# Opening of a two-layer hybrid decoder trunk: the first half's first projections on h times the norm weight, the norm factor multiplied into the products, and 44 matmuls on a constant ahead

## The chip, the cores and the metric

The kernel runs on one core of a Trainium2 chip. TensorE (PE in the profile; PEld is its weight load) multiplies matrices into PSUM, eight banks of 512 float32 numbers per partition. VectorE (DVE), ScalarE (ACT) and GpSimd (POOL) work on tiles of 128 partitions; SyncE (SP) issues transfers. The engines run beside each other and wait for each other by semaphores; each takes its own instructions in order. The metric is the device time of one execution in microseconds, lower is better.

## The reference

Two layers, each a mixer and a feed-forward sub-layer with RMS norms around both. 16 learned tokens are put ahead of 512, so L = 528 and D = 1024. The part that the change touches is the head of the first mixer:

```python
def rms_norm(x, g):
    y = xf * lax.rsqrt(jnp.mean(xf * xf, axis=-1, keepdims=True) + RMS_EPS)
    return y * g
...
u = rms_norm(h, pre_g)
z = jnp.einsum("bld,de->ble", u, w_in)
q, k, v, f_logit, a_val, a_gate, sc_b, sc_c, sc_x = jnp.split(z, idx, axis=-1)
...
a = a_val * jax.nn.sigmoid(a_gate)
a = causal_depthwise_conv(a, a_dw_w) + a_dw_b
...
y_sc = sc_b * causal_depthwise_conv(sc_c * sc_x, sc_conv_w)
```

The rest of a layer is an attention with forget gates (8 heads), a head norm, an output projection, a post norm, and a gated feed-forward part with a short convolution; everything is computed in float32.

## The kernel before

All activations lie transposed: a tile `[128, 8, 528]` holds feature 128 k + p in partition p and block k. `h` is such a tile. The 528 tokens are worked in two halves of H = 264; `hf` is the half. To get float32 accuracy, both operands of a product are split into a high part (rounded by a cast) and a low part (the rest), and each product is three matmuls, high x high, low x high, high x low (`mm3`). `uhi` and `ulo` are the two parts of the normed input u, `whi` and `wlo` those of a weight block of 128 output columns (8 x 128 x 128 numbers, 512 KB; `raw` is the loaded block, in a ring of three buffers). A weight block costs a transfer on SP's queue, a cast on ACT (L617) and a subtraction on DVE (L621); its raw buffer is free when the subtraction is done.

The order of all instructions is set while the program is built, by a planner (`Flow`): work is handed to it with a duration, a priority and what it waits for, and it lets each engine take what can start first, by priority among what is ready. PE is fed by generators ("threads") that yield what they wait for. The resulting order on each engine is fixed in the program.

The opening, under the pool `pre`, does this in the kernel before:

- `load_h` asks for h in four transfers for each half (pairs of blocks k), weight blocks 0, 1 and 2 come between the halves, the next ones as raw buffers come free. The parameters of both layers (`pv`) are two transfers on POOL's queue; DVE makes `pg` from each (L407).
- ACT squares pairs of blocks of h (`Norms.square`, L723), DVE adds them up, and PE multiplies the sum with a matrix of 1/D (`om_d`, L772), which gives the mean square in all partitions. ACT and DVE make the factor of it (L782 to L793).
- ACT multiplies h with the norm weight into `hg` (`gained`, L802), DVE multiplies by the factor (L814), ACT casts to `uhi` (L816) and DVE subtracts to `ulo` (L817), pair by pair.
- `first_half` then runs the first six weight blocks on the first half: blocks 0 and 1 together, k by k, then 2, 3, 4 and 5 together. Blocks 0 and 1, and 2 and 3, are gate and value of the two tiles of the convolution module, 4 and 5 are `sc_c` and `sc_x` of the short convolution.

The mixer starts with `gated` for the first half (the sigmoid by exp, ln and exp on ACT, then a product with the value on DVE into `apad`), runs the same six blocks on the second half (`firsts`: 0 and 1, then 2 and 3, then 4 and 5), and starts the 31 taps of the convolution on DVE (`tap`, L932). Behind these 288 first products comes the value projection (L1183), and from there projections, attention and convolution are interleaved.

Of the kernel before, what the change touches and what calls it, by code (L numbers as in the profile page):

```python
# [13 lines left out]
ALU = mybir.AluOpType  # L14
# [35 lines left out]
NP = 6  # L50

# [304 lines left out]
def tile_hybrid_trunk(ctx: ExitStack, tc: tile.TileContext, xT, wflat, pv_d, out):  # L356
# [46 lines left out]
    for l in range(DEPTH):  # L403
        pv = T(const, [P, NPV], F32, f"pv{l}")
        nc.gpsimd.dma_start(pv, pv_d[l])
# [254 lines left out]
    class First:  # L660
# [8 lines left out]

        def steps(self, hf, *group):  # L670
# [218 lines left out]
    def mixer(l, ypool, first, close_first, spans):  # L889
# [7 lines left out]

        mp = ms.enter_context(tc.tile_pool(name=f"mp{l}", bufs=1, reuse_waits="tile"))
# [6 lines left out]
        conv, apads, sigs = [], [], []  # L905
        for j in range(2):
            sigs.append(T(mp, [P, L], F32, ("sccx", "cxp")[j]))
            apad = T(mp, [P, L + CK - 1], F32, "apad", 2)
            nc.gpsimd.memset(apad[:, :CK - 1], 0.0)
            apads.append(apad)  # L910
            conv.append(T(mp, [P, L], F32, "cacc", 2))
        gated_at = {}

        def gated(hf, j, tok):
            c = half_sl(hf)
            sig = sigs[j][:, c]
            us = act_us(H)
            a = a0 = act(us, lambda: nc.scalar.activation(sig, first.ps[hf, 2 * j], AF.Exp, scale=-1.0), tok)
            b = act(us, lambda: nc.scalar.activation(sig, sig, AF.Ln, bias=c_one), a)
            b = act(us, lambda: nc.scalar.activation(sig, sig, AF.Exp, scale=-1.0), b)  # L920
            gated_at[hf, j] = got = dve(dve_us(H), lambda: nc.vector.tensor_mul(
                apads[j][:, CK - 1 + H * hf:CK - 1 + H * (hf + 1)], first.ps[hf, 2 * j + 1], sig), b, prio=0)
            for i in range(2):
                first.slot[hf, 2 * j + i].close(a0, got)
# [31 lines left out]
        for j in range(2):  # L956
            gated(0, j, first.tok[0, 2 * j + 1])
# [6 lines left out]
        def sc_c(j):  # L964
            t = sc[j] = T(mp, [P, L], F32, "sccx")

            def use(hf, ps, tok):
                c = half_sl(hf)
                sc_at[j, "c", hf] = act(act_us(H), lambda: nc.scalar.copy(t[:, c], ps), tok)
                return [sc_at[j, "c", hf]]  # L970

            return use

        def sc_x(j):
            t = sc[j]
            cx = T(mp, [P, L + 2], F32, "cxp")
# [37 lines left out]
        for i, make in ((4, sc_c), (5, sc_x)):  # L1014
            use = make(0)
            for hf in range(2):
                evacs += use(hf, first.ps[hf, i], first.tok[hf, 5])
# [935 lines left out]
```

## Time and profile before

| what | value |
|---|---|
| median of 3 runs | 1320.25 us (1317.92 to 1321.16) |
| the profiled execution | 1320.06 us |
| its span, first to last instruction | 1318.4 us |
| mean granted clock of TensorE | 0.997 |
| PE busy | 1278.1 us, 97% of the span |
| DVE, ACT, POOL busy | 859.1, 626.3, 98.9 us |
| bytes moved by the transfers | 118.26 MB, mean 90 GB/s |

A row of the timeline has the start and the duration in microseconds, the engine, the line of the kernel, the instruction, its output and inputs with their shapes, and how often it stands there in a row (then the duration is that of all); behind it, in brackets, the idle time of the engine and what ended it. A matmul's duration covers its way through the array, and matmuls overlap, so the distance between starts says how fast they go. A row on a line or tile has the shortest, the median and the longest duration in ns.

### The profile page before, as it was taken

Reading aid. Unit: us, or ns where it says so; the run is one execution under the profiler, and the core shown is the slowest. Engines: PE = TensorE matmul, PEld = TensorE weight load, DVE = VectorE, ACT = ScalarE, POOL = GpSimd, SP = SyncE. Lnnn points to the kernel's source line nnn. Section 1 sums busy time; section 2 is a strip of 40 time slices with the busy share of each in tenths; the row PEclk is TensorE's granted clock in tenths of the full one; section 3 lists DMA queues with packets and bytes.
Section 4 is the critical chain, followed back from the end, with each engine's and each line's share of the span. In section 5 each row is a group of like instructions: output and inputs, shape, how many; then the busy total and the mean of one; then the engine's idle time right before and its main releaser. Section 6 shows DMA issues by size and latency. Waiting matters only on the chain. (4 is left out here: it accounts for less than half of the span.)

```text
span 1318.4 us, 23824 instructions
## 1 busy us (share of the span) xinstructions
PE 1278.1 (97%) x9758; PEld 1223.3 (93%) x9758; DVE 859.1 (65%) x1450; ACT 626.3 (48%) x1176; POOL 98.9 (8%) x255
## 2 busy tenths in 40 slices
PE   5999999999999999999989999999999999999997
PEld 4989898999999999999989898979999799989997
DVE  6588856488633674576575888666877247646764
ACT  7345568555423432234662555685644233323353
POOL 1313321000000000000003223110000000000000
PEclk9999999999999999999989999999999999999999
DMA  7032120602222222223240322116032222232221
GB/s 247 21 98 75 56 75 33 213 30 85 92 97 81 97 86 91 96 86 106 82 163 17 99 82 65 57 54 214 24 97 85 92 97 95 71 108 97 90 71 65
DMA packets 42700, 118.26 MB, mean 90 GB/s; under 512 B 4848, under 2 KB 15088, under 8 KB 42592
## 3 DMA queue, kind: packets, MB, share of 16 engines
q1 hardware_dynamic: 42496, 116.48, 26.6%
q8 instruction: 77, 1.26, 0.4%
q0 software_dynamic: 96, 0.26, 0.1%
q14 instruction: 31, 0.25, 0.1%
HBM read 108.04 MB, written 4.33 MB: 85 GB/s over the span
## 5 line engine op out<-in xcount | busy, mean ns | idle before, releaser
L648 PE MATMUL psum<-uhi,whi 128*128 128x264 f32 (+1 forms) x1984 | 466.9, 288 | 7.4 <-ACT uhi L816 7.4
L648 PE MATMUL psum<-ulo,whi 128*128 128x264 f32 (+1 forms) x1984 | 461.7, 285 | 0.9 <-DVE ulo L817 0.9
L648 PE MATMUL psum<-uhi,wlo 128*128 128x264 f32 (+1 forms) x1984 | 459.7, 284 | 0.0
L648 PEld LDWEIGHTS psum<-uhi,whi 128*128 128x128 f32 x1984 | 333.4, 189 | 11.6 <-ACT uhi L816 8.6
L648 PEld LDWEIGHTS psum<-ulo,whi 128*128 128x128 f32 x1984 | 334.2, 190 | 1.9 <-DVE ulo L817 1.5
L648 PEld LDWEIGHTS psum<-uhi,wlo 128*128 128x128 f32 x1984 | 334.0, 190 | 0.0
L648 PE MATMUL psum<-yhi,whi 128*128 128x264 f32 (+3 forms) x840 | 235.2, 304 | 1.4 <-ACT yp L1885 1.0
L648 PE MATMUL psum<-ylo,whi 128*128 128x264 f32 (+3 forms) x840 | 232.6, 300 | 1.0 <-DVE ylo L1085 0.8
L648 PE MATMUL psum<-yhi,wlo 128*128 128x264 f32 (+3 forms) x840 | 231.7, 299 | 0.5 <-DVE wlo L621 0.5
L503 ACT CAST whi<-raw 128x1024 fp32r<-128x1024 f32 (+1 forms) x110 | 113.5, 1033 | 212.5 <-PE psum L648 198.9
L504 DVE TENSOR_TENSOR wlo<-raw,whi 128x1024 fp32r<-128x1024 f32 (+1 forms) x110 | 132.0, 1201 | 81.5 <-ACT whi L503 79.5
L648 PEld LDWEIGHTS psum<-yhi,whi 128*128 128x128 f32 x840 | 150.0, 188 | 10.2 <-ACT yp L1885 1.4
L648 PEld LDWEIGHTS psum<-ylo,whi 128*128 128x128 f32 x840 | 150.0, 188 | 7.5 <-DVE ylo L1085 2.0
L648 PEld LDWEIGHTS psum<-yhi,wlo 128*128 128x128 f32 x840 | 150.2, 188 | 6.1 <-DVE wlo L621 0.9
L1834 DVE SCALAR_TENSOR_TENSOR c<-z,pv,c 128x528 f32<-128x528 f32 (+1 forms) x176 | 132.2, 757 | 2.7
L621 DVE TENSOR_TENSOR wlo<-raw,whi 128x1024 fp32r<-128x1024 f32 (+2 forms) x86 | 102.5, 1207 | 43.0 <-ACT whi L617 42.5
L617 ACT CAST whi<-raw 128x1024 fp32r<-128x1024 f32 (+2 forms) x86 | 87.9, 1035 | 35.8 <-DMA raw<-in_w_dram 17.4
L932 DVE SCALAR_TENSOR_TENSOR cacc<-apad,pv,cacc 128x528 f32<-128x528 f32 x120 | 87.6, 773 | 0.5
L1852 ACT CAST yhi<-c 128x528 fp32r<-128x528 f32 (+1 forms) x44 | 27.6, 628 | 111.3 <-DVE c L1848 111.3
L1844 ACT ACTIVATE c<-c 128x528 f32<-128x528 f32 (+1 forms) x44 | 28.2, 640 | 81.7 <-DVE c L1834 81.7
L1832 ACT ACTIVATE c<-z,pv 128x528 f32<-128x528 f32 (+1 forms) x88 | 63.5, 728 | 0.0
L1797 DVE TENSOR_TENSOR z<-psum,rz 128x528 f32<-128x528 f32 x40 | 28.3, 709 | 53.7 <-PE psum L648 52.1
(199 smaller groups left out, 1422.1 us busy)
## 6 DMA issues: line engine op xcount, KB each, us to landing
raw<-in_w_dram SPq DMA_DIRECT2D x160, 512.0 KB
raw<-in_w_dram SPq DMA_DIRECT2D x32, 448.0 KB
h<-in_x_dram SPq DMA_DIRECT2D x16, 264.0 KB
raw<-in_w_dram SPq DMA_DIRECT2D x4, 528.0 KB
q<-q SPq DMA_DIRECT2D x16, 132.0 KB
k<-k SPq DMA_DIRECT2D x16, 132.0 KB
h_dram<-h SPq DMA_DIRECT2D x4, 528.0 KB
h<-h_dram SPq DMA_DIRECT2D x8, 264.0 KB
```

Of the source, the lines that this page charges most:

```text
L503: nc.scalar.copy(hi[:, :sz], raw[:, :sz])
L504: nc.vector.tensor_sub(lo[:, :sz], raw[:, :sz], hi[:, :sz].bitcast(F32))
L617: nc.scalar.copy(box["hi"][:, :sz], box["raw"][:, :sz])
L621: nc.vector.tensor_sub(lo[:, :sz], box["raw"][:, :sz], box["hi"][:, :sz].bitcast(F32))
L648: nc.tensor.matmul(d, lhsT=w[a][:, k, cols], rhs=rhs(b, k, hf), start=start and i == 0 and p == 0, stop=stop and i == n - 1 and p == 2)
L932: nc.vector.scalar_tensor_tensor(conv[j], in0=src, in1=conv[j], scalar=col("a_dw_w", CK * j + i), op0=ALU.mult, op1=ALU.add)
L1797: nc.vector.tensor_mul(two(t[:, off:]), srcs[0], two(rz))
L1832: nc.scalar.activation(dst, src[:, 2:2 + 2 * fw], AF.Copy, scale=wtap(2, t))
L1834: nc.vector.scalar_tensor_tensor(dst, in0=src[:, i:i + 2 * fw], scalar=wtap(i, t), in1=dst, op0=ALU.mult, op1=ALU.add)
L1844: silu = nc.scalar.activation(cs[0], cs[0], AF.Silu)
L1852: nc.scalar.copy(ghi, cs[0])
```

## The change

The first half's projections no longer wait for the norm factor. u = h x gain x factor, and the factor is one number for each token, thus for each column of the product; so the first half's six blocks are multiplied with the two parts of h x gain, and the factor `rz0` is multiplied into the products afterwards.

- High and low parts of h x gain for the first half are made straight from h, block by block: ACT scales into the high part, DVE takes the low part in one operation (`yhi`, `ylo`; they lie in tiles of the later `y`). The pool of these tiles and a new pool `mq0` are opened ahead.
- The six blocks run one after the other over all k (`First.alone`) instead of two or four together.
- `gated` and the use of `sc_c` multiply with `rz0` on DVE (lines 925, 932 and 1005 and 1006 of the changed kernel). `gated` for the first half is planned in the opening.
- u itself is still needed in both halves for later projections: DVE multiplies h by gain and factor in one operation per block (L1821), ACT casts (L1825) and DVE subtracts (L1827). The buffer `hg` is gone.
- 44 matmuls on a tile of ones stand at the head of PE's queue; the planner is told 8.0 us for them. Nothing reads their result.
- Layer 0's `pv` goes on SP's queue ahead of all, and weight block 0 ahead of h.

```diff
-        nc.gpsimd.dma_start(pv, pv_d[l])
+        (nc.gpsimd if l else nc.sync).dma_start(pv, pv_d[l])
...
+        def alone(self, hf, both, *ids):
+            slots = [(yield from flow.grab(pring[0]["mm" if both else "s"], self.slot[hf, ids[0]]))]
...
+            for j, i in enumerate(ids):
...
+                yield [self.ws[i].tok]
+                for k in range(KD):
+                    yield [When(lambda: self.at.get((hf, k)))]
+                    mm3({hf: self.ps[hf, i]}, self.ws[i].w, [k], self.rhs, start=k == 0, stop=k == KD - 1)
...
+        def gated(self, hf, j, tok, rz=None, rz_at=None):
...
+            if rz is not None:
+                a = b = dve(dve_us(H), lambda: nc.vector.tensor_mul(sig, gate, rz), tok, rz_at, prio=0)
...
+            if rz is not None:
+                b = dve(dve_us(H), lambda: nc.vector.tensor_mul(sig, sig, rz), b, prio=0)
...
+        warm = T(sp, [P, H], F32R, "warm", 1)
+        nc.vector.memset(warm.bitcast(F32), 1.0)
+        for i in range(WARM):
+            nc.tensor.matmul(psum[:, 7, :H], lhsT=warm[:, :P], rhs=warm, start=True, stop=True)
+        flow.pe += WARM_US
+        plan_w(1, -1)
         h, h_at = load_h(sp, xT)
...
-        hg, hg_at = T(sp, [P, KD, L], F32, "hg", 1), {}
+        for k in range(KD):
+            hk, hi, lo, gc = h[:, k, :H], u_raw[0][k], u_raw[1][k], g0[:, k:k + 1]
+            c = act(act_us(H) + 0.06, lambda hk=hk, hi=hi, gc=gc: nc.scalar.activation(hi, hk, AF.Copy, scale=gc),
+                    h_at[0, k - k % 2], prio=0)
+            d = dve(stt_us(H), lambda hk=hk, hi=hi, lo=lo, gc=gc: nc.vector.scalar_tensor_tensor(
+                lo, in0=hk, scalar=gc, in1=hi.bitcast(F32), op0=ALU.mult, op1=ALU.subtract), c, prio=0)
+            first.at[0, k] = [c, d]
...
+        def normed(hf, prio):
+            c = half_sl(hf)
+            key = ("h", hf)
+            yield from norms.factor(key, H, out=None if hf else rz0)
...
+        def opening():
+            for j in range(2):
+                yield from first.alone(0, True, 2 * j, 2 * j + 1)
+                front.gated(0, j, first.tok[0, 2 * j + 1], rz0, rz_at)
+            for i in (4, 5):
+                yield from first.alone(0, False, i)
...
-        flow.thread(first_half(first, False))
+        flow.thread(normed(0, 1.2))
+        flow.thread(normed(1, 0.7))
+        flow.thread(opening())
```

Where instructions stand now. On PE, the head of the queue before (`om_d` is the matrix of the mean, 161 and 168 are weight blocks 0 and 1):

```order
L772 MATMUL psum_67<-acc_137,om_d_88 128x264 x2
L648 MATMUL psum_67<-uhi_113,whi_161 128x264
L648 MATMUL psum_67<-ulo_114,whi_161 128x264
L648 MATMUL psum_67<-uhi_113,wlo_166 128x264
L648 MATMUL psum_67<-uhi_113,whi_168 128x264
```

and in the changed kernel (`whi_218` is weight block 0, `yhi_22` and `yhi_23` the high parts for k = 0 and 1):

```order
L1790 MATMUL psum_67<-warm_159 128x264 x44
L650 MATMUL psum_67<-yhi_22_126,whi_218 128x264
L650 MATMUL psum_67<-ylo_30_134,whi_218 128x264
L650 MATMUL psum_67<-yhi_22_126,wlo_224 128x264
L650 MATMUL psum_67<-yhi_23_127,whi_218 128x264
L650 MATMUL psum_67<-ylo_31_135,whi_218 128x264
```

The sum for the norm factor stood ahead of all products; now it stands in the middle of block 2, and that of the second half behind the first three products of block 4.

On DVE, between the second half's sum of squares and the second half's low parts, before:

```order
L732 TENSOR_TENSOR acc_189<-acc_189,c_261 128x528
L621 TENSOR_TENSOR wlo_314<-raw_243,whi_310 128x1056
L621 TENSOR_TENSOR wlo_331<-raw_272,whi_316 128x1056
L787 SCALAR_TENSOR_TENSOR rs_23_129<-psum_67,rs_23_129 128x264
L793 SCALAR_TENSOR_TENSOR rs_23_129<-rs_23_129 128x264
L814 TENSOR_TENSOR hg_130<-hg_130,rs_23_129 128x2x264 x3
L817 TENSOR_TENSOR ulo_114<-hg_130,uhi_113 128x2x264 x3
```

and in the changed kernel (`rz_44` is the first half's factor, `rs_47` the second half's; `sccx` and `cxp` hold the sigmoids of the two tiles):

```order
L623 TENSOR_TENSOR wlo_405<-raw_331,whi_393 128x1056
L925 TENSOR_TENSOR sccx_145<-psum_67,rz_44_153 128x264
L925 TENSOR_TENSOR cxp_149<-psum_67,rz_44_153 128x264
L802 SCALAR_TENSOR_TENSOR rs_47_206<-psum_67,rs_47_206 128x264
L1821 SCALAR_TENSOR_TENSOR h_205<-h_205,pg_3_70,rz_44_153 128x264
L808 SCALAR_TENSOR_TENSOR rs_47_206<-rs_47_206 128x264
L1821 SCALAR_TENSOR_TENSOR h_205<-h_205,pg_3_70,rz_44_153 128x264
L932 TENSOR_TENSOR sccx_145<-sccx_145,rz_44_153 128x264
L932 TENSOR_TENSOR cxp_149<-cxp_149,rz_44_153 128x264
L933 TENSOR_TENSOR apad_146<-psum_67,sccx_145 128x264
L933 TENSOR_TENSOR apad_150<-psum_67,cxp_149 128x264
L1821 SCALAR_TENSOR_TENSOR h_205<-h_205,pg_3_70,rs_47_206 128x264 x4
```

The first half's gating and its first two scalings of u moved in ahead of the second half's u, which begins with the last row. The remaining scalings and low parts of the first half's u stand behind those of the second half.

On SP's queue, the head before:

```order
L460 DMA h_128<-in_x_dram 128x2x264 x4
L613 DMA raw_135<-in_w_dram 128x1024
L613 DMA raw_140<-in_w_dram 128x1024
L613 DMA raw_147<-in_w_dram 128x1024
L460 DMA h_128<-in_x_dram 128x2x264 x4
```

and in the changed kernel:

```order
L407 DMA pv_2_68<-in_pv_dram 128x254
L615 DMA raw_207<-in_w_dram 128x1024
L462 DMA h_205<-in_x_dram 128x2x264 x4
L615 DMA raw_213<-in_w_dram 128x1024
L615 DMA raw_221<-in_w_dram 128x1024
L462 DMA h_205<-in_x_dram 128x2x264 x4
```

The parameters and weight block 0 moved ahead of h. Behind the value projection's first matmul PE has the same order in both programs.

119 lines of the change are left out of this document (81 added, 38 removed).

## The prediction

> **What bounds the kernel now.** I read first the busy times by stretch (columns: stretch, its length, then busy time and number of instructions of PE, the weight load, DVE, ACT and POOL, clock, share and rate of the DMAs).
>
> ```profile
> span 1318.4 us, 23824 instructions
> ...
> 17.00:22.20 5.20, 4.53 (x19) 4.23 (x20) 5.20 (x8) 5.20 (x9) 0.00 (x0) 1.00 0.24 88
> 22.20:55.50 33.30, 33.30 (x271) 33.17 (x271) 20.22 (x30) 15.58 (x32) 3.41 (x11) 1.00 0.29 97
> 55.50:120.00 64.50, 62.58 (x480) 58.79 (x480) 52.41 (x122) 27.62 (x68) 19.29 (x44) 1.00 0.25 68
> ...
> 22.20:1318.40 1296.20, 1271.46 (x9737) 1217.94 (x9736) 845.64 (x1431) 608.32 (x1147) 94.61 (x230) 1.00 0.26 87
> ```
>
> From 22.2 us on PE is busy 1271.46 of 1296.20 us; in the first projections (22.2 to 55.5) it never rests and takes 33.30/271 = 0.123 us a matmul, in the mixer's first part it works 62.58 of 64.50 us. What is late is its start: 19 matmuls in the 5.2 us before 22.2, where 42 would go. The timeline of PE shows that (start, duration, what; idle time before it):
>
> ```profile
> 17.07 0.59 PE L648 MATMUL psum<-uhi,whi 128*128 128x264 f32 x1 [6.31 <-ACT uhi L816]
> 18.26 0.59 PE L648 MATMUL psum<-ulo,whi 128*128 128x264 f32 x1 [0.60 <-DVE ulo L817]
> ...
> 21.51 0.42 PE L648 MATMUL psum<-uhi,whi 128*128 128x264 f32 x1
> 21.73 0.42 PE L648 MATMUL psum<-ulo,whi 128*128 128x264 f32 x1
> ...
> 22.17 0.36 PE L648 MATMUL psum<-uhi,whi 128*128 128x264 f32 x1
> ...
> 22.48 0.28 PE L648 MATMUL psum<-uhi,wlo 128*128 128x264 f32 x1
> 22.61 0.28 PE L648 MATMUL psum<-uhi,whi 128*128 128x264 f32 x1
> ...
> 56.07 0.28 PE L1183 MATMUL psum<-whi,uhi 128*128 128x264 f32 x1
> ```
>
> The first product starts at 17.07 us, after the norm factor. Until 22.17 matmuls start 0.22 us apart, afterwards 0.12: the array runs at half rate for 5.1 us from the first of them, 3.9 from 18.26, where they become dense. All 288 first products are done when L1183, the value projection, starts at 56.07. From there the order of every engine is the same in both programs, but for some DVE and ACT rows at the border and one convolution tap. So the gain is how much earlier the changed kernel reaches that matmul, less what the mixer loses.
>
> **The change: when the data are there.** The transfers go through one queue, in another order. Rate and sizes:
>
> ```profile
> 0.00:6.30 6.30, 0.00 (x0) 0.00 (x0) 0.48 (x2) 2.98 (x4) 4.30 (x25) 1.00 0.69 226
> 6.30:12.00 5.70, 2.10 (x4) 1.17 (x4) 3.16 (x5) 4.99 (x9) 0.00 (x0) 1.00 1.04 391
> ...
> h<-in_x_dram SPq DMA_DIRECT2D x8, 264.0 KB
> raw<-in_w_dram SPq DMA_DIRECT2D x4, 512.0 KB
> pv<-in_pv_dram POOLq DMA_DIRECT2D x2, 127.0 KB, 3.7
> ...
> 4.71 0.19 DVE L407 TENSOR_SCALAR pg<-pv 128x42 f32<-128x42 f32 x1 [4.71 <-DMA pv<-in_pv_dram]
> ...
> 6.32 1.33 ACT L723 ACTIVATE c<-h 128x528 f32<-128x528 f32 x2 [0.34 <-DMA h<-in_x_dram]
> ...
> 23.03 0.33 SPq L613 DMA_DIRECT2D raw<-in_w_dram  x1
> ...
> 27.47 1.08 ACT L617 CAST whi<-raw 128x1056 fp32r<-128x1056 f32 x1 [0.61 <-DMA raw<-in_w_dram]
> ```
>
> The third pair of h landed at 6.3 us, behind 3 x 264 + 2 x 127 = 1046 KB. In the changed order the first pair stands behind 127 + 512 + 264 KB and the other pv on POOL's queue, 1030 KB: about 6.2 us, where nothing else was waiting. The next pairs follow 0.7 us apart at 391 GB/s, faster than ACT takes them. Both layers' pv must be in before DVE goes on (its third row waits for the second one, still on POOL's queue): one of them was in at 4.71 us here, DVE's first low part is due at 6.7, so I take nothing for it. Weight block 3, the first to reuse a raw buffer, comes behind all of h: 254 + 2112 + 4 x 512 KB are 4.52 MB; 226 GB/s x 6.3 us are 1.42 MB, and the rest at 391 GB/s ends at 14.2 us. By 6.3 us 1.42 MB had moved and 1.07 had been used as landed, 0.9 us of transfer at 391 GB/s; so block 3 lands near 15.1. A reload by itself (528 KB) took from 23.03 to 27.47, 4.4 us; those are blocks 4 and 5, issued near 13.3 and 14.5.
>
> **The change: the work on ACT and DVE.** Durations of the nearest rows:
>
> ```profile
> 7.56 1.72 ACT L802 ACTIVATE hg<-h,pg 128x264 f32<-128x264 f32 x4
> ...
> 9.18 1.03 ACT L617 CAST whi<-raw 128x1024 fp32r<-128x1024 f32 x1
> ...
> L866 DVE SCALAR_TENSOR_TENSOR ulo<-h,pg,uhi x32: 471/489/495, 268.0 to 940.2; 128x264 fp32r<-128x264 f32 x24, 128x250 fp32r<-128x250 f32 x8
> ...
> 21.73 2.35 DVE L621 TENSOR_TENSOR wlo<-raw,whi 128x1024 fp32r<-128x1024 f32 x2
> ...
> 24.00 2.33 DVE L732 TENSOR_TENSOR acc<-acc,c 128x528 f32<-128x528 f32 x3
> ...
> 34.18 1.94 DVE L817 TENSOR_TENSOR ulo<-hg,uhi 128x528 fp32r<-128x528 f32 x3
> ...
> 657.80 1.05 PE L772 MATMUL psum<-acc,om_d 128*128 128x264 f32 x4
> 658.49 0.48 PE L648 MATMUL psum<-yhi,whi 128*128 128x264 f32 x1
> ...
> 30.46 0.43 ACT L785 ACTIVATE rs<-rs 128x264 f32<-128x264 f32 x1
> ...
> 40.35 0.42 DVE L921 TENSOR_TENSOR apad<-psum,cxp 128x264 f32<-128x264 f32 x1
> ```
>
> So: a scaled high part 0.43 us, a low part about 0.46 in a row, a weight's high part 1.03, its low part 1.18, an add 0.77, a pair of u low parts 0.65, a sum of squares on PE (four passes, with the slower matmul behind it) 0.9. Squares are 1.33/2 = 0.65. In the new order:
>
> - Removed on ACT: 16 scalings of hg (L802), 6.9 us; added 8 high parts, 3.4. Removed on DVE: 8 multiplications by the factor (L814); added 8 low parts, 16 scalings by gain and factor (L1821) and 6 small products (L925, L932, and two at L1005): about 8 x 0.46 + 16 x 0.46 + 6 x 0.4 = 13.4 us against 8 x 0.65 = 5.2. DVE gets 8 us more in the first 42.
> - First block: ACT makes two high parts by 7.1, the first weight by 8.1, six high parts by 10.7, weights 1 and 2 by 11.7 and 12.7. DVE ends the first weight's low part at 9.3, the last low part of h at 12.1, weights 1 and 2 at 13.3 and 14.5. PE's third product waits until 9.3, block 0 goes at DVE's pace to 12.5, block 1 waits for 13.3 and ends at 16.0.
> - The 44 constant matmuls start near 1.1 us (a memset first; DVE has nothing before it). All cold they end at 1.1 + 44 x 0.22 = 10.8, all fast at 6.4; with 4 to 5 cold us as in the rows above, near 8.6. All lie before 9.3 or nearly, so they cost nothing, and the products behind them run fast. If all were cold, block 0 would end at 13.7 instead of 12.5, and block 1, held until 13.3 anyway, 0.4 us later.
> - ACT then squares: three by 14.6, waits for block 3 (15.1, cast by 16.1), the fourth by 16.7. DVE splits block 3 by 17.3 and ends the sum at 18.1; PE is there at 17.8 and loses 0.3. Sum 0.9, block 2 ends at 20.1, block 3 at 23.0. The second half's sum (DVE, behind blocks 4 and 5, 23.1) follows three products later; block 4 ends at 26.9, block 5 at 29.8. No wait for weights: the last is split near 22.3.
> - **The new wait.** The second half's u needs its factor. PE's sum ends at 24.3; three ACT operations of 0.43 (with hand-over 1.6) to 25.9; DVE does the factor and two scalings by 28.0, while ACT runs the gating's six operations to 25.9 + 6 x 0.43 = 28.5; four products of 0.42 stand in DVE's queue ahead of the second half's u and end at 29.7; four scalings end at 31.6, and the first low part at 32.2. PE stands from 29.8 to 32.2: 2.4 us. Behind it on DVE come 4 x 0.46 + 4 x 0.65 us and more, so that the last pair is split at 36.8; blocks 0 and 1 of the second half end at 36.8 + 12 x 0.12 = 38.3, the other 96 products at 38.3 + 96 x 0.123 = 50.1.
>
> So the value projection starts near 50.1 instead of 56.07: 6.0 us. Parts: the start 17.07 - 9.3 = 7.8 earlier; 2.7 of cold clock and gaps that go (39.0 us before for what takes 288 x 0.123 + 0.9 = 36.3); 0.5 for four products done ahead of the two waits for weights. Less 0.9 for the first half's sum, which now stands among products, 0.4 for block 0's pace, 0.8 and 0.3 for the waits, 2.4 at the seam, 0.2 for the pace behind it: 11.0 - 5.0.
>
> **Given back later.** DVE does eight taps between the last gating and the value projection as before, with a shorter time for them, and comes out some 2 us later against PE. It had room:
>
> ```profile
> 63.57 0.17 DVE L1172 TENSOR_TENSOR fx<-psum,pv 128x8 f32<-128x8 f32 x1 [5.10 <-POOL p L413]
> ```
>
> DVE sat 5.1 us there for POOL's memsets, which begin behind the same gating (0.4 us later against PE by my times). I take 0.2 off: 5.8 us. The profiled run took 1320.06 us (span 1318.4), 0.19 under the median; from the median, 1320.25 - 5.8 = **1314.4 us**. The bounds: with no wait at the seam, 9.3 + 288 x 0.123 + 1.8 = 46.5, gain 9.6, 1310.7; with the chain 4 us later, gain 1.8, 1318.5.
>
> **The clock at the new gap.** Such a gap has cost more than itself in this trace:
>
> ```profile
> 665.78 1.16 PE L772 MATMUL psum<-acc,om_d 128*128 128x264 f32 x4 [2.23 <-DVE acc L732]
> 668.03 0.59 PE L648 MATMUL psum<-uhi,whi 128*128 128x264 f32 x1 [1.09 <-ACT uhi L816]
> ...
> 668.00:672.00 4.00, 3.71 (x15) 3.42 (x16) 3.96 (x8) 4.00 (x8) 0.00 (x0) 0.50 0.00 0
> ```
>
> After 2.23 us idle, 1.16 of work and 1.09 idle the granted clock was 0.50. The Trainium skill (TensorE: Matmul & The Clock Gate, "Why this matters for your kernels") states that only gaps over about 3 us send the array back to half rate; by that rule a gap of 2.4 us leaves the clock alone and the sum stays 1314.4. The trace speaks against the rule, though it had two gaps close together. The same page gives about 3.4 us of sustained work as what raises the clock; the 3.9 dense us above agree with it.
>
> **Rivals.**
> 1. The wait at the seam is mostly gone, because ACT and DVE hand over faster than my row by row sum: 1310.7 to 1312.5. For it: I took each row with its whole length, and neighbours on an engine overlap a little. Against: DVE's rows stand nearly without gaps from 6.8 to 36.8 us.
> 2. The reloads are late. ACT's queue holds block 3's cast ahead of five squares, so a late landing moves both factors. If block 3 takes 4.4 us from the end of h (13.8), it lands at 18.2 and all moves by 3.1: 1317.5, no change to be told.
> 3. The clock falls at the seam: the 48 products after it run cold for up to 5.1 us; 24 of them take 5.3, the rest 2.9: 40.5 instead of 38.3, so 1316.6.
> 4. The constant matmuls don't raise the clock: products stay cold until about 16 us, block 1 ends 3 us later, of which the seam hides a part: 1315.5 to 1317.4.
> 5. Slower: the reloads of blocks 3, 4 and 5 each hold ACT, one after another, since a buffer comes free only behind DVE's split. It decides from 9.8 us of such waits in all, 3.3 a block; at 4.4 a block 1314.4 + 13.2 = 1327.6. Against: the one such wait of ACT that I found in the opening is the 0.61 us of the row at 27.47.
>
> **How the numbers follow.** Forecast 0.50 (its own range 1312.5 to 1316.2), rival 1: 0.15, 2: 0.14, 3: 0.07, 4: 0.05, 5: 0.09. About 0.3% (4.0 us, so 1316.3) is what a measurement here can tell from no change. Faster: 0.50 + 0.15 + 0.02 of rival 4 = 0.67; within 0.3%: 0.14 + 0.07 + 0.03 = 0.24; slower: 0.09. The range 1310.7 to 1318.6 leaves out rival 5 and the edges of 1 and 2.
>
> **What would show it.** Right: PE's third real product near 9.3 us waiting for DVE's `wlo`; products 0.12 us apart from there; PE waiting near 30 us, about 2.4 us, for `uhi` or `ulo`; the value projection near 50. Wrong: idle ACT before the cast of block 3 beyond 0.5 us; clock 0.50 after 30 us; or a value projection near 50 with an end less than 4 us earlier, which would put the loss in the mixer.

## The result

| | kernel before | changed kernel |
|---|---|---|
| median, same chip, first pair | 1320.25 us (7 executions, 1317.46 to 1323.27) | 1312.06 us (7, 1310.68 to 1315.81) |
| ratio, 95% interval | | 0.9943 (0.9929 to 0.9957) |
| second and third time it was measured, each beside the kernel before | 1320.20, 1321.30 us | 1312.95, 1311.73 us; ratios 0.9942 (0.9926 to 0.9957), 0.9933 (0.9917 to 0.9950) |
| profiled execution, and its span | 1320.06, 1318.4 us | 1311.54, 1309.8 us |
| value projection begins (profile) | 56.07 us | 49.55 us |

The change makes the kernel 8.2 us faster; 5.8 had been forecast. The busy times of the changed kernel by stretch (same columns as in the prediction):

```profile
9.00:13.00 4.00, 3.52 (x27) 3.10 (x26) 4.00 (x9) 4.00 (x8) 0.00 (x0) 1.00 1.05 383
13.00:31.20 18.20, 16.54 (x126) 15.89 (x126) 15.69 (x27) 14.30 (x27) 0.00 (x0) 1.00 0.64 209
31.20:49.50 18.30, 17.83 (x144) 17.63 (x145) 16.93 (x31) 7.15 (x15) 3.67 (x9) 1.00 0.19 60
49.50:114.00 64.50, 63.25 (x483) 59.30 (x482) 53.25 (x125) 27.64 (x69) 18.79 (x45) 1.00 0.24 67
```

From 9 us on DVE and ACT have no pause in the first stretch, and PE stands 1.7 us in the second. The timeline of PE in the changed kernel shows where:

```profile
1.26 7.84 PE L1790 MATMUL psum<-warm 128*128 128x264 f32 x44 [1.26 <-DVE warm L1788]
8.94 0.28 PE L650 MATMUL psum<-yhi,whi 128*128 128x264 f32 x1
...
9.48 0.39 PE L650 MATMUL psum<-yhi,wlo 128*128 128x264 f32 x1
...
13.04 0.39 PE L650 MATMUL psum<-yhi,wlo 128*128 128x264 f32 x1 [0.38 <-DVE wlo L623]
...
18.69 1.13 PE L787 MATMUL psum<-acc,om_d 128*128 128x264 f32 x4 [0.90 <-DVE acc L747]
...
31.30 0.39 PE L650 MATMUL psum<-uhi,whi 128*128 128x264 f32 x1 [0.82 <-ACT uhi L1825]
32.06 0.39 PE L650 MATMUL psum<-ulo,whi 128*128 128x264 f32 x1 [0.38 <-DVE ulo L1827]
...
49.55 0.28 PE L1222 MATMUL psum<-whi,uhi 128*128 128x264 f32 x1
```

Three waits are left: for block 1's low part, for the first half's sum, and the seam between the halves, where the last product of the first half starts at 30.19 us and the next would have at 30.31; it starts at 31.30, and the second one 0.64 us later than its pace: 1.63 us. On ACT, in the same profile, the one long wait is for weight block 3:

```profile
15.62 1.05 ACT L619 CAST whi<-raw 128x1024 fp32r<-128x1024 f32 x1 [1.49 <-DMA raw<-in_w_dram]
```

**Where the lead comes from.** The same matmul starts earlier in the changed kernel than in the kernel before: this lead is 6.5 us at the value projection and 6.3 at 72 us, so 0.2 us are given back there, and DVE still sits idle for POOL:

```profile
57.13 0.17 DVE L1211 TENSOR_TENSOR fx<-psum,pv 128x8 f32<-128x8 f32 x1 [4.82 <-POOL p L415]
```

At 79 us the lead is 7.2. In the profile of the kernel before PE waits there for a transfer:

```profile
86.10 0.34 PE L1333 MATMUL psum<-k,q 128*16 128x16 f32 x2 [0.75 <-DMA k<-sq]
```

By 90 us 6.9 of it are left, so of this wait about 0.55 us stay. At 253 us the lead rises by 1.1 to 8.0, where PE in the kernel before waits 0.85 us for a sum of squares (at 260 us there). At the end it is 8.5. What of this growth behind the opening belongs to the change is the subject of the first experiment.

### The profile page after: what moved, and what is told of

The parts are those of the page before. It is cut to its first block, busy times and chain, and to the rows that moved or that the text cites. A ratio compares the mean times of both kernels' runs of the same rounds, so it can differ in the third digit from the quotient of the medians.

```text
span 1309.8 us, 23934 instructions
## 1 busy us (share of the span) xinstructions
PE 1282.9 (98%) x9802; PEld 1228.0 (94%) x9802; DVE 865.1 (66%) x1473; ACT 621.2 (47%) x1167; POOL 97.7 (7%) x254
## 3 DMA queue, kind: packets, MB, share of 16 engines
q8 instruction: 77, 1.26, 0.4%
## 5 line engine op out<-in xcount | busy, mean ns | idle before, releaser
L650 PE MATMUL psum<-uhi,whi 128*128 128x264 f32 (+1 forms) x1936 | 451.5, 287 | 1.9 <-ACT uhi L831 1.1
L650 PE MATMUL psum<-ulo,whi 128*128 128x264 f32 (+1 forms) x1936 | 446.7, 285 | 0.5 <-DVE ulo L1827 0.4
L650 PE MATMUL psum<-uhi,wlo 128*128 128x264 f32 (+1 forms) x1936 | 444.8, 284 | 0.0
L650 PEld LDWEIGHTS psum<-uhi,whi 128*128 128x128 f32 x1936 | 322.9, 189 | 5.8 <-issue 2.4
L650 PEld LDWEIGHTS psum<-ulo,whi 128*128 128x128 f32 x1936 | 323.8, 189 | 1.4 <-DVE ulo L1827 0.6
L650 PEld LDWEIGHTS psum<-uhi,wlo 128*128 128x128 f32 x1936 | 323.7, 189 | 0.0
L650 PE MATMUL psum<-yhi,whi 128*128 128x264 f32 (+3 forms) x888 | 249.6, 304 | 1.5 <-ACT yp L1978 1.0
L650 PE MATMUL psum<-ylo,whi 128*128 128x264 f32 (+3 forms) x888 | 245.6, 299 | 1.0 <-DVE ylo L1124 0.8
L650 PE MATMUL psum<-yhi,wlo 128*128 128x264 f32 (+3 forms) x888 | 245.5, 299 | 1.0 <-DVE wlo L623 0.9
L650 PEld LDWEIGHTS psum<-ylo,whi 128*128 128x128 f32 x888 | 159.3, 188 | 7.6 <-DVE ylo L1124 2.0
```

Of the source, the lines that this page charges most:

```text
L650: nc.tensor.matmul(d, lhsT=w[a][:, k, cols], rhs=rhs(b, k, hf), start=start and i == 0 and p == 0, stop=stop and i == n - 1 and p == 2)
```

## Experiments

**The same kernels again.** Nothing edited: the changed kernel twice, the kernel before once.

> The changed kernel once more, nothing altered. It asks whether what came behind the opening belongs to the change: in the first profile the changed kernel was 6.5 us ahead of the kernel before at the value projection and 8.6 us at the end. Theory A (it belongs to the change): the value projection's first matmul stands at 49.5 us (49.3 to 49.8) again, and the span is 1309.8 us (1309.4 to 1310.3) again. Theory B (the later 2 us are of one execution): the value projection stands at 49.5 us again, but the span comes out between 1310.5 and 1312.5 us, and the places at which the lead grew (a wait for a DMA near 80 us, one for a sum of squares near 255 us, the low clock near 660 us) read otherwise.

> The kernel before once more, nothing altered, for its profile. Three executions of the changed order (two of the changed kernel, one without the constants) reach the value projection at 49.2 to 49.6 us and end with spans of 1309.7 to 1312.7 us; the 3 us between the spans arise where the granted clock falls to 0.50 for one stretch of 3.41 us, at other places in each execution. Theory A: the kernel before has the same lottery. It reaches the value projection at 56.1 us again (55.8 to 56.3), and its span moves from 1318.4 by about 1.4 us for each such fall more or less; the wait for a DMA of k at 86 us (0.7 us) and the one for a sum of squares at 260 us (0.85 us) may be there or not. Theory B: these two waits and the clock's pattern belong to the order of the kernel before; both waits come again, and the span is 1318.4 us within 0.5.

> The changed kernel a third time, nothing altered, as the measure for the three runs beside it, since the time of one execution depends on how many stretches of low clock it meets. Expected from the two profiles of it: value projection at 49.3 to 49.6 us, one fall of 6.83 us near 658 us and none to two of 3.41 us (near 202, 727 and 857 us), 1.4 us each; median 1311.5 to 1313.5 us. If instead its opening moves by more than 0.5 us, differences of that size between the other kernels mean nothing.

The changed kernel reached the value projection at 49.31 and 49.45 us, with spans of 1312.7 and 1308.8. The opening repeats, the rest does not: both spans lie outside the 1309.4 to 1310.3 us of theory A. The clock records of the traces (start of a stretch and its length in us, granted clock) say why:

```
changed kernel       6.26 651.95 1.0   658.20 6.83 0.5   665.03 641.71 1.0
the same, again      6.78 651.95 1.0   658.72 6.83 0.5   665.55  61.44 1.0   726.99 3.41 0.5
                   730.40 126.29 1.0   856.69 3.41 0.5   860.11 450.56 1.0
the same, third      4.82 655.36 1.0   660.18 3.41 0.5   663.59 645.12 1.0
```

Every length is a multiple of 3.413 us (191, 2, 188; 18, 1, 37, 1, 132; 192, 1, 189); the third met 3.41 us of low clock where 6.83 had been expected. The second execution lost 1.5 us to the third near 728 us and 1.6 more near 857, by these two falls. The same stretch of work, from 726.5 to 731 us, in the first and in the second execution:

```profile
726.50:731.00 4.50, 4.36 (x35) 4.07 (x36) 4.45 (x9) 1.38 (x4) 0.00 (x0) 1.00 0.65 192
```

```profile
726.50:731.00 4.50, 4.50 (x25) 4.20 (x26) 3.76 (x7) 1.39 (x4) 0.00 (x0) 0.62 0.46 153
```

The kernel before, again, reached the value projection at 57.57 us, 1.50 later than in its first profile, and had a span of 1318.6. ACT's rows of its opening show the cause of the larger part:

```profile
6.55 0.64 ACT L723 ACTIVATE c<-h 128x528 f32<-128x528 f32 x1 [0.45 <-DMA h<-in_x_dram]
7.99 0.64 ACT L723 ACTIVATE c<-h 128x528 f32<-128x528 f32 x1 [0.80 <-DMA h<-in_x_dram]
```

The last pair of h came 1 us later (both squares could run from 6.32 us in the first profile); the sum moved from 8.66 to 9.52 us, the first product from 17.07 to 17.92, and the clock rose 6.7 us behind that product instead of 5.3. Theory A holds for the wait at 260 us, which was not there, and B for the wait on k: 0.77 us again, at 87.61, and 0.79 in the experiment with constants below; in ten of the eleven profiles of the changed kernel and of its variants it is absent, in one it is 0.32. Why k's transfers land sooner in the new order was not tried.

So of the 8.2 us, 6.5 to 8.3 are the opening (56.07 and 57.57 against 49.55, 49.45 and 49.31), 0.2 go back, and of the wait for k that goes 0.55 stay. The rest differs from execution to execution: the wait at 260 us, and how many clock falls are met. Executions with the same mean clock differ by about 8 us: at 0.999 the spans are 1308.7 and 1308.8 against 1316.2 to 1317.5, at 0.994 they are 1312.7 to 1313.1 against 1320.4 to 1321.7.

**Without the constants.**

```diff
-WARM, WARM_US = 44, 8.0
+WARM, WARM_US = 0, 8.0
```

> The changed kernel without the 44 matmuls on a constant; the order of all other work is the same and nothing else is left out. Theory: TensorE then starts cold at 8.9 us and its products stand 0.22 us apart instead of 0.12 until the clock rises, some 5 us after the first product (it rose 5.0 us after the first constant in the changed kernel). About 22 products of block 0 cost 0.1 us more each, so the projection of blocks 0 and 1 ends some 2 us later; the wait of 0.9 us for a sum of squares at 17.8 us and the seam's 1.6 us swallow part of it. The value projection begins 0.5 to 1.5 us later than with the constants (50.0 to 51.0 us), and the time is 1312.6 to 1313.6 us where the changed kernel has 1312.1. Rival 1: block 0 is paced by VectorE's lower parts anyway (0.42 us for each chunk of three products), so the time does not move by more than 0.3 us. Rival 2: all 2.2 us or more reach the value projection: 1314.3 us or above.

Measured: 1312.09 us (1310.73 to 1314.22), ratio to the kernel before 0.9939 (0.9926 to 0.9952), value projection at 49.23 us. PE's timeline:

```profile
9.20 0.59 PE L650 MATMUL psum<-yhi,wlo 128*128 128x264 f32 x1 [0.45 <-DVE wlo L623]
...
12.45 0.40 PE L650 MATMUL psum<-ylo,whi 128*128 128x264 f32 x1
12.67 0.30 PE L650 MATMUL psum<-yhi,wlo 128*128 128x264 f32 x1
...
13.79 0.28 PE L650 MATMUL psum<-yhi,wlo 128*128 128x264 f32 x1
...
18.27 1.09 PE L787 MATMUL psum<-acc,om_d 128*128 128x264 f32 x4
...
30.93 0.39 PE L650 MATMUL psum<-uhi,whi 128*128 128x264 f32 x1 [0.83 <-ACT uhi L1825]
```

Until the clock rose at 12.69 us the dense products stood 0.22 us apart (this is what cold means here), and block 1's third product came at 13.79 instead of 13.04 us: 0.75 us lost. But PE then arrived at the first half's sum when it was ready, and had no wait there, where the changed kernel has 0.90. The loss went into a wait that was there anyway. The theory named this wait but let too much past it; rival 1 had the time right for another reason (block 0 was not paced by DVE). The 44 matmuls are worth nothing in this order.

**Constants alone, in the kernel before.** 40 at PE's head and 48 behind the first half's sum.

```diff
+            s["t_at"] = [Tok(flow.pe)]
...
+        if between is not None:
+            yield [When(lambda: between[0].get("t_at"))]
+            between[1](48)
...
+        constants(40)
```

> The kernel before with constants alone: 40 matmuls on a constant at the head of TensorE's work and 48 more behind the first half's sum of squares, so that the clock is up when the first product comes at 17.07 us; the norm and the products stay as they were. Theory: 18 products from 18.26 us on stand 0.12 us apart instead of 0.22, so the value projection begins 1.0 to 1.9 us earlier (54.2 to 55.1 us instead of 56.07), time 1318.3 to 1319.2 us where the kernel before has 1320.2. Then the constants are worth more in the old order than in the new one, where taking them out cost nothing. Rival: as in the changed kernel nothing is gained, because later waits (the second half's sum of squares on VectorE, the low parts of the weights) hold TensorE: the value projection stays at 56.1 us within 0.3. A third: the constants stand in the way of the first sum of squares at 8.66 us and the value projection is later, 56.4 us or above.

Measured: 1317.63 us, the kernel before beside it 1321.43, ratio 0.9971 (0.9960 to 0.9983). PE's timeline:

```profile
9.79 1.13 PE L772 MATMUL psum<-acc,om_d 128*128 128x264 f32 x4 [2.12 <-DVE acc L732]
10.57 7.67 PE L1752 MATMUL psum<-warm 128*128 128x264 f32 x48
18.08 0.28 PE L648 MATMUL psum<-uhi,whi 128*128 128x264 f32 x1
18.66 0.39 PE L648 MATMUL psum<-ulo,whi 128*128 128x264 f32 x1 [0.30 <-DVE ulo L818]
...
54.64 0.28 PE L1184 MATMUL psum<-whi,uhi 128*128 128x264 f32 x1
```

The sum in the kernel before, in its first profile:

```profile
8.66 2.10 PE L772 MATMUL psum<-acc,om_d 128*128 128x264 f32 x4 [8.66 <-DVE acc L732]
```

From the start of the first half's sum to the value projection it takes 44.85 us, against 47.41 and 48.05 in the two profiles of the kernel before (sums at 8.66 and 9.52): 2.6 to 3.2 us. The value projection came where the theory had it, but the gain has two parts, of which the theory named one. 0.7 us come between the sum and the second product (8.87 us apart against 9.60 and 9.59): the sum now runs at full clock, 1.13 us long instead of 2.10. Behind the second product 1.8 us are gained against the first profile (35.98 against 37.81), the 18 products of the theory, and 2.5 against the other one, in which the clock rose later. The first product is itself held up by the constants, by some 0.6 us (the cast before it starts at 16.78 us, and in the kernel before the product follows the start of the cast by 0.69), which costs nothing, since the second one waits for `ulo` until 18.66 us anyway. So constants do pay, where PE's own pace sets the time of the products. In the changed kernel the gain of the opening is the products' place ahead of the norm: from 54.64 to 49.4 us.

**The old order of the transfers.**

```diff
-        (nc.gpsimd if l else nc.sync).dma_start(pv, pv_d[l])
+        nc.gpsimd.dma_start(pv, pv_d[l])
...
-        plan_w(1, -1)
```

> The changed kernel with the transfers in the old order: the first half of h ahead of weight block 0, and the first table of small parameters on GpSimd's queue again; nothing is left out. The order of the squares and casts on ScalarE follows from it. Theory: the third product waits for the low part of block 0, which is 1.0 us later (10.3 to 10.6 us), but block 0 then runs 0.12 us a product since all its low parts of h are there, so block 1 ends at 16.0 to 16.5 us as before, and the value projection begins at 49.1 to 49.7 us: the transfer order is worth nothing by itself, 1312 to 1313 us. Rival 1: everything behind it is later by the full 1.0 us (value projection at 50.3 us or above). Rival 2: the first half's squares, which come earlier in this order, bring both norm factors forward, and the seam shrinks: 48.7 us or less.

Measured: 1312.69 us (1311.54 to 1312.97), the changed kernel beside it 1311.73; value projection at 50.30 us. PE's timeline, and its stretches:

```profile
10.70 0.39 PE L650 MATMUL psum<-yhi,whi 128*128 128x264 f32 x1 [2.07 <-ACT whi L619]
11.96 0.49 PE L650 MATMUL psum<-yhi,wlo 128*128 128x264 f32 x1 [0.75 <-DVE wlo L623]
...
32.50 0.28 PE L650 MATMUL psum<-ylo,whi 128*128 128x264 f32 x1
32.74 0.29 PE L650 MATMUL psum<-uhi,whi 128*128 128x264 f32 x1
```

```profile
8.70:12.00 3.30, 0.55 (x3) 0.34 (x3) 2.50 (x5) 3.30 (x5) 0.00 (x0) 1.00 1.04 397
12.00:16.40 4.40, 4.40 (x24) 4.40 (x25) 4.19 (x6) 4.40 (x8) 0.00 (x0) 0.61 0.93 331
```

The third product came 2.5 us later, not 1.0 (PE had waited 2.07 us for the first weight and 0.75 for its low part), and behind that pause the clock fell to 0.50 from 12.09 to 15.51 us. Yet only 0.9 us reached the value projection, because the squares stand earlier in this order, both factors were there in time and the seam had no wait. That is rival 1's place with part of rival 2's mechanism. The transfer order is worth 0.9 us of the gain.

**Block 3 without its late buffer.** It gets a raw buffer of its own, so that its transfer goes ahead of the second half of h.

```diff
-            box["raw"] = T(wp, [P, CHUNK], F32, "raw", 3)
+            box["raw"] = T(sp, [P, CHUNK], F32, "rawx", 1) if own else T(wp, [P, CHUNK], F32, "raw", 3)
```

> The changed kernel with a raw buffer of its own for weight block 3, so that its DMA no longer waits for a buffer to come free and goes ahead of the second half of h; nothing is left out. Theory: ScalarE's wait of 1.49 us for raw block 3 (it landed at 15.59 us) goes, and with it TensorE's 0.90 us at 17.8 us; the value projection begins 0.5 to 0.9 us earlier (48.6 to 49.0 us), time 1311.3 us where the changed kernel has 1312.1. Rival: the second half of h lands later by the block's 1.3 us, its sum of squares with it, and the seam wait grows by what is saved: the value projection stays at 49.5 us or moves to 50.5, time 1312.1 to 1313.1 us.

Measured: 1316.23 us, ratio 0.9973 (0.9962 to 0.9984), value projection at 53.41 us. It is 3.9 us worse than the changed kernel there. ACT's row, and PE's:

```profile
16.64 1.05 ACT L621 CAST whi<-raw 128x1024 fp32r<-128x1024 f32 x1 [2.86 <-DMA raw<-in_w_dram]
```

```profile
21.33 2.10 PE L790 MATMUL psum<-acc,om_d 128*128 128x264 f32 x4 [2.23 <-DVE acc L750]
...
35.16 0.39 PE L653 MATMUL psum<-uhi,whi 128*128 128x264 f32 x1 [1.98 <-ACT uhi L1828]
```

Block 3 was in time, but its place in ACT's queue was taken by block 4, whose cast stood ahead of three squares and waited 2.86 us. The first half's sum came at 21.33 instead of 18.69 us, PE's clock fell during the 2.23 us (0.50 from 21.03 to 24.44), and the seam grew. The rival's direction was right; its mechanism was not, and the loss was larger than it allowed. The run shows what a late reload ahead of the squares costs: 2.6 us at the sum, 3.9 at the value projection.

**The squares ahead of block 3's cast.**

```diff
-        plan_w(FIRST["ffn_w_down"], 0.2)
+        plan_w(3, 0.2)
+        plan_w(FIRST["ffn_w_down"], 0.45)
```

> The changed kernel with the cast of weight block 3 and later ones ranked behind the first half's squares on ScalarE: the fourth square stands ahead of the cast that waited 1.49 us for its DMA. Nothing is left out and no transfer moves. Theory: the first half's sum is complete before TensorE asks for it, TensorE's wait of 0.90 us for it goes, both norm factors come 0.6 to 0.9 us earlier and the seam does not grow: value projection at 48.6 to 49.0 us instead of 49.3 to 49.55, time 1311.5 us where the changed kernel has 1312.1 to 1312.9. Rival: the saved 0.9 us comes back as a longer wait at the seam, because the second half's sum now stands 6 products later in TensorE's order: value projection at 49.3 to 49.6 us.

Measured: 1314.26 us (1314.0 to 1315.6; the kernel before beside it 1321.43), ratio 0.9947 (0.9934 to 0.9960), value projection at 49.00 us. PE has no wait for the first half's sum any more; its seam:

```profile
30.75 0.39 PE L650 MATMUL psum<-uhi,whi 128*128 128x264 f32 x1 [1.32 <-ACT uhi L1826]
31.51 0.39 PE L650 MATMUL psum<-ulo,whi 128*128 128x264 f32 x1 [0.38 <-DVE ulo L1828]
```

0.90 us saved, 0.50 lost at the seam (2.13 us there instead of 1.63): half of the theory, half of the rival. Behind it the profiled execution lost 3.1 us to the third of the changed kernel by clock falls at 727 and 856 us, and all five executions of this run have a mean clock of 0.993 to 0.995; so the median is no measure of the 0.3 to 0.55 us gained at the value projection.

**The seam.** The second half's scalings stand ahead of the first half's gating products on DVE.

```diff
-        flow.thread(normed(1, 0.7))
+        flow.thread(normed(1, -0.5))
```

> The changed kernel with the second half's normalised chunks put ahead, on VectorE, of the first half's gating products; nothing is left out. Theory: the seam wait (0.8 us for uhi and 0.4 us for ulo, with what else TensorE stands still there some 1.6 us) is there because VectorE works at the gating products before it makes u; with the order turned round the wait is gone and the value projection begins at 48.2 us (47.9 to 48.7) instead of 49.5, time 1310.8 us where the changed kernel has 1312.1. Rival: u cannot come sooner, since it waits for the second half's own sum of squares (its last matmul at 24.0 us) and ScalarE's casts, or the pairs of the second half wait for the gating products to give PSUM back: the wait changes its name and the value projection stays at 49.5 us within 0.3, time within 0.3 us of the changed kernel.

Measured: 1312.23 us (1311.15 to 1314.83), value projection at 49.15 us:

```profile
30.93 0.39 PE L650 MATMUL psum<-uhi,whi 128*128 128x264 f32 x1 [0.21 <-ACT uhi L1825]
31.67 0.39 PE L650 MATMUL psum<-ulo,whi 128*128 128x264 f32 x1 [0.35 <-DVE ulo L1827]
```

```profile
29.27 1.08 ACT L619 CAST whi<-raw 128x1056 fp32r<-128x1056 f32 x1
```

The seam shrank from 1.63 to 1.00 us and no further: with the gating products out of the way the scalings on DVE start at 28.30 us instead of 29.69, but ACT casts a weight block (29.27 to 30.35) before it comes to `uhi`. Both theory and rival were half right: two waits stood one behind the other. The 0.3 us by which this run is ahead of the third profile of the changed kernel at the value projection are gone by 140 us, where it is 0.15 behind.

**The gap between the layers.** 10 matmuls of the constant matrix with itself, 128 wide, written into the sum's own bank ahead of it. In the first try they stood ahead of another sum:

```diff
+                for _ in range(self.fill if j == 0 and key == ("h", 1) else 0):
+                    nc.tensor.matmul(ps[:, :P], lhsT=om_d, rhs=om_d, start=True, stop=True)
```

> The changed kernel with 10 matmuls of one constant matrix with itself, 128 wide, put on TensorE ahead of the sum of squares that it waits 2.23 us for between the two layers (at 658.0 us in the changed kernel); nothing is left out and no other order changes. Theory: the granted clock falls there because TensorE is busy only 0.35 of the 3.41 us before it; with the gap filled the fall of 6.83 us at 658 does not come, the sum takes 1.1 instead of 1.3 to 2.0 us and some 16 matmuls after 661 us stand 0.12 us apart instead of 0.22: 1.5 to 2.2 us in all, time 1310.2 us where the changed kernel has 1312.1 to 1312.9. Rival: the clock falls all the same (the 1.09 us gap that follows is enough, or what matters is not how busy TensorE is), and the time is that of the changed kernel, or up to 0.5 us longer where the filling delays the sum.

The fall at 658 us came as before, and the row behind shows what was measured instead, the price of ten such matmuls (20 rows in the profile) where nothing waits: 2.2 us (1315.95 us in all).

```profile
675.10 2.39 PE L787 MATMUL psum<-om_d 128*128 128x128 f32 x20
677.33 1.06 PE L789 MATMUL psum<-acc,om_d 128*128 128x264 f32 x4
```

In the second try the key is `("y", 1)`.

> The experiment of filling the gap between the layers, with the 10 matmuls at the place meant: ahead of the sum of squares that TensorE waits 2.23 us for near 658 us (in the first try they stood ahead of a later sum, near 675 us, that nothing waited for, and cost their own 2.1 us). Theory: TensorE is then busy through the 3.41 us that end at 658, the fall of 6.83 us does not come, the sum takes 1.1 us instead of 1.3 to 2.0, and 16 matmuls after 661 us stand 0.12 us apart instead of 0.22. The lead over the changed kernel, matmul by matmul, is 0 up to 655 us and 1.5 to 2.2 us from 667 us on; the median is 1.5 to 2.2 us under that of the changed kernel beside it. Rival: the clock falls all the same, by the gap of 1.09 us behind the sum, or the filling delays the sum: lead of 0 or below.

Measured: 1311.70 us (1309.26 to 1312.38), the changed kernel beside it 1311.73; the profiled execution has a span of 1307.8 us and no fall at all from 5.37 to 1305.85 us. Its stretches at the gap, and then those of the changed kernel's first profile:

```profile
655.60:658.00 2.40, 2.40 (x22) 2.27 (x21) 2.09 (x5) 2.16 (x7) 0.00 (x0) 1.00 0.99 340
658.00:661.00 3.00, 1.60 (x6) 0.86 (x5) 3.00 (x6) 2.75 (x6) 0.00 (x0) 1.00 0.20 83
661.00:665.00 4.00, 3.85 (x31) 3.85 (x32) 3.97 (x8) 3.82 (x7) 0.00 (x0) 1.00 0.00 0
```

```profile
655.60:658.00 2.40, 0.18 (x2) 0.00 (x0) 2.15 (x5) 2.16 (x6) 0.00 (x0) 1.00 0.87 307
658.00:661.00 3.00, 1.97 (x4) 1.02 (x4) 2.42 (x4) 1.93 (x5) 0.00 (x0) 0.53 0.27 108
661.00:665.00 4.00, 3.78 (x15) 3.48 (x16) 3.82 (x7) 4.00 (x9) 0.00 (x0) 0.50 0.00 0
```

31 matmuls instead of 15 in the four microseconds behind 661. In all twelve profiles without this filling the clock fell here, in this one it did not; that it stays up whenever the gap is filled is not shown, and the next experiment speaks against it. The size depends on the execution: 2.1 us ahead of the changed kernel's first profile, 1.0 of its third, which had only one stretch of 3.41 us there. Against the spread by the other falls that is too little to move a median of five.

**Three edits together** (the squares first, the seam, the filled gap).

> Three edits together on the changed kernel: the fourth square ahead of block 3's cast, the second half's normalised chunks ahead of the gating products on VectorE, and the 10 matmuls in the gap between the layers; nothing is left out. Theory: the first two add, because one removes TensorE's wait for the first half's sum (0.9 us) and the other what it turned into at the seam (1.7 us in that run): value projection at 47.9 to 48.6 us instead of 49.3 to 49.6, and with the gap filled 2.5 to 3.5 us under the changed kernel beside it, 1309 to 1310 us. Rival: what is gained at the opening is lost behind it, because the gating products and with them the convolution's taps come later on VectorE: the lead of 1 us at the value projection shrinks to under 0.3 us by 140 us, and only the filled gap is left (1.5 to 2.2 us).

Measured: 1311.39 us (1308.85 to 1313.56), the changed kernel beside it 1311.73. Value projection at 48.55 us, 0.9 us ahead of the changed kernel as the theory had it; at 140 us 0.4 of it are left, near the rival's 0.3. In its profile the fall between the layers still came, though later and for 3.41 us (661.84). Behind the filled gap PE waits 1.09 us and 0.46 us more for u; here both fell into one stretch of 3.41 us, in which PE was busy for 1.86, while the execution with the filling alone had 2.29 in the stretch behind the filled one. The three edits together are not measurably faster; no version tried is.

## Why the prediction was right

The side, the range (1310.7 to 1318.6) and the likeliest mechanism held. The time was 2.3 us too high: 1312.06 us lies below the forecast's own 1312.5 to 1316.2 and among the times of rival 1, though what rival 1 asked for, a seam with hardly a wait, did not come.

- **Start and block 0.** Third product at 9.3 forecast, 9.43 to 9.48 us measured; block 1's wait to 13.3, measured 13.04. Right.
- **Constants.** They ended at 9.1 us instead of 8.6, cost nothing, and the clock was up at 6.26 us. But the 2.7 us "of cold clock and gaps that go" were put down as part of the gain: without the constants 0.75 us of cold clock appear and vanish in the wait for the sum. The forecast's own line for constants without effect, 0.4 us at block 1, was nearer than rival 4, which had charged 1 to 3 us for products that stay cold until 16 us; in the run without constants they were cold until 12.69 us, and nothing of it reached the value projection.
- **Block 3.** Landing at 15.1 forecast, 15.59 us measured; ACT's wait 0.5 forecast, 1.49 measured, since ACT was through its three squares at 14.1 us and not 14.6; PE's wait for the sum 0.3 forecast, 0.90 measured. The prediction had named more than 0.5 us of idle ACT there as a sign of being wrong; the sign came, and it cost PE 0.6 us more than worked out. This was rival 2's mechanism at a small size; the run with block 4's cast in the way gives its price at a large one.
- **The seam**, the term that the forecast turned on: 2.4 us forecast, 1.63 measured. The chain on DVE was right (first low part complete at 32.2 forecast, 32.0 measured); PE came to it 0.5 us later than worked out. The value projection was put at 50.1 and stood at 49.55: the opening gave 6.5 us instead of 6.0. The seam is not the cause of these 0.5 us, since the second product behind it came at 32.06 us and so only 0.14 earlier than forecast; 0.4 us come from behind it: the forecast had PE follow the splits of u there until 36.8 us, and the trace has no such wait (blocks 0 and 1 end at 37.85 us instead of 38.3).
- **Given back later.** 0.2 us, as forecast, with 4.8 us of DVE's room left. The step that failed is what the forecast took to be the end of it: that the rest of the program is a copy. PE's wait of 0.75 us for k is gone in the new order, of which 0.55 us stay, and the profile of before already had its row.
- **The sum against one profile.** The opening of the kernel before was taken at 56.07 us, and a second profile has 57.57. The kernel before waits for all four pairs of h before its first sum, so a late transfer moves everything; the changed kernel's opening moved by 0.24 us in three profiles. The gain forecast was that over an execution with an early h; how often h is late, two profiles don't tell.
- **The clock at the new gap** (rival 3). It did not fall at the seam. PE was busy 2.22 of the 3.41 us there:

```profile
30.15:33.56 3.41, 2.22 (x16) 1.80 (x15) 3.41 (x9) 1.36 (x3) 0.00 (x0) 1.00 0.01 2
```

How PE's busy time and the clock go together is the subject of the last section. The forecast of no fall came out right without the reason.

## What to carry to other kernels

A norm factor that is one number for each column of a product can be multiplied in afterwards; what that buys here is not the cold clock but the wait for the whole input. The opening also moved less from one execution to the next (0.24 us in three profiles against 1.50 in two); whether it would bear a late last transfer of h was not tried. Before paying for warm-up matmuls, look for the next wait behind the cold stretch: where one is as long as the loss, they buy nothing, and where PE's pace sets the time they bought 2.6 to 3.2 us here. Removing one wait in a chain of neighbours returned half of it at most: 0.3 to 0.55 of 0.90 us ahead of the sum, and at the seam 0.6 of 1.63, of which nothing was left at 140 us. In one run it cost 3.9 us. The rest reappeared in the next wait.

## What the runs showed of the hardware

The clock is decided on a grid. In 14 profiles every stretch between two changes of the granted clock is a multiple of 3.413 us, and the grid's place against the program's start differs from one execution to the next: in the eleven profiles with constants at PE's head the first constant starts at 1.26 or 1.27 us, and the clock rose 3.0 to 6.2 us behind it. Cutting the traces on that grid and leaving out the last 8 us of each, the clock fell behind 25 stretches. In 20 of them PE was busy for 0.64 to 1.92 us of the 3.41; in the other five for 2.13 to 2.15. It stayed up behind every stretch with 2.16 us or more, and behind some with 2.01 to 2.15 and one with 1.91; so the border lies between 0.56 and 0.63 of the stretch, as far as this profile's busy time can tell. The last 8 us do not fit: there the clock fell behind a stretch with 1.32 us, but stayed up behind three with 1.54 to 1.69, so busy time alone does not settle it. The clock needed more to rise than to stay up: in eleven of the falls PE was busy for 2.07 to 2.90 us of the first low stretch and the clock stayed low for a second one, and wherever it rose PE had been busy for 2.97 us or more. In none of the 25 was a single idle time of PE longer than 2.3 us. The same work near 725 us, in the first profile of the changed kernel and in the second, cut at another place:

```profile
723.06:726.47 3.41, 2.05 (x16) 1.73 (x14) 3.17 (x10) 1.45 (x3) 0.00 (x0) 1.00 0.91 269
```

```profile
723.58:726.99 3.41, 1.88 (x14) 1.30 (x13) 3.19 (x10) 0.81 (x2) 0.00 (x0) 1.00 0.84 283
```

The first kept the clock, the second lost it for 3.41 us, and 1.4 us of time. With up to three such stretches more or less, this is most of the spread of 5 us between executions of one kernel (spans of 1308.7 us at a mean clock of 0.999 and of 1312.7 to 1313.1 at 0.994). The Trainium skill (TensorE: Matmul & The Clock Gate, "Part 1: The HAM clock gate") states a free-running window of 3413 ns; the traces agree. The Trainium skill's rule for keeping the clock, no idle gaps over about 3 us (same page, "Why this matters for your kernels"), is not enough here. PE's two waits in the stretch that lost the clock, in the second execution, were these:

```profile
724.51 0.41 PE L1255 MATMUL psum<-fpre,ones_r 128*128 128x40 f32 x2 [0.82 <-DVE fpre L1250]
726.43 0.71 PE L1264 MATMUL psum<-ident,gt 128*8 128x128 f32 x5 [0.70 <-DVE gt L1256]
```
